# A hybrid attention block on one core: softmax sums applied to the outputs of group A instead of to its weights

## The chip, the cores and the metric

The kernel runs on one core of one Trainium2 chip. The metric is device time in microseconds, the median of several executions. The core has a matrix engine (PE, with its weight loads shown apart as PEld), a vector engine (DVE), an activation engine (ACT), a slow general engine (POOL) and a queue of transfers (SP). Matmuls write to PSUM, which is cut into banks of 512 float32 columns; ACT and DVE read them from there.

## The reference

One layer on a sequence of 1024 frames and 1024 channels, in float32. Group A (8 heads of width 64) is a chunked softmax attention, group B (8 heads) a stick-breaking attention. Both are normalised, concatenated, projected and added to the input; then comes a gated feed-forward part with a short convolution. The part that the change touches is the softmax of group A:

```
scores = einsum('bnqhd,bnkhd->bnhqk', qc, kb) * D ** -0.5
scores = where(valid, scores + bias, NEG_INF)
p = softmax(scores, axis=-1)
o = einsum('bnhqk,bnkhd->bnqhd', p, vb)
...
mixed = concatenate([rmsnorm(ya, norm_a_g), rmsnorm(yb, norm_b_g)], axis=-1)
x = x + mixed @ w_out
```

A softmax is an exponential divided by its row sum. The division may be made on the weights `p` (up to 640 for each query row and head) or on the outputs `o` (64 for each row and head); the result is the same up to rounding.

## The kernel before

The whole program runs its matmuls on PE in an order that the program itself writes out. Stages follow one another: the projections, group B, group A, the output projection, the feed-forward part. Groups A and B are latency chains between PE, DVE and ACT, so independent matmuls are put in between them, called the filler: a generator `filler()` that yields, three matmuls at a time, first the q and k projections of later head pairs (`q_p`, `k_p`, line 151), and then the half of the output projection that belongs to group B (`pb`, also line 151). The filler of the output projection comes in two halves of two weight tiles each; the second half is held back by

```
while at["qk"] < 6:
    yield None
```

and `at["qk"]` becomes 6 only when the last of the four head pairs of group A begins. What filler is left after the last block runs before the projection of group A (`pa`, line 151) starts.

A planner (`flow`) sets the order on each engine. It keeps a model clock: PE work moves the clock on (`flow.work`), chains of ACT, DVE, POOL and transfer work are emitted when the model says that their inputs are there, and when PE needs a chain that the model says is not done, `ready()` takes filler until it is. Besides, `run()` spends a planned amount of filler after each block: `cur.cost * RATES_A[p]`, where the costs of the eight blocks of a head pair add up to one, so `RATES_A` is the microseconds of filler in a head pair.

Group A has four head pairs p and eight blocks i of 128 queries in each; nk, the number of 128-key pieces, is 5, 5, 5, 5, 4, 3, 2, 1. A block goes through three steps. `scores(h)`, for each of two heads: matmuls into a bank pair (`sa`, L1058 and L1059), bias added by DVE (L1072), row maximum (L1075), exponential on ACT with the row sum as a by-product (L1089), reciprocal of the sum (L1092), and the product of the weights with it, on DVE for head 0 (L1083) and on ACT for head 1 (L1082). `turn(h)`: the weights are transposed by PE (`tpa`, L1110) and copied out by ACT (`pta`, L1114). `output`: matmuls with v (`yy`, L1123), 2 nk of them in a block. Two blocks share one bank `yy`, of which they use the first 256 columns; DVE copies these out (`yq`, L1533). The transposes and `yy` take turns in two banks. Block b's scores are issued with the transposes of block b-1 and, every other block, with the outputs of blocks b-3 and b-2.

After the last block ACT and DVE square the outputs, PE sums them (`na_ms`, L1138), ACT takes a root (with a table load, L1627), DVE a reciprocal, and PE spreads the result over the partitions (`na_rb`, L181); the `pa` results wait for that. The output weights arrive one after another through one raw tile `wo_r`: transfer, high part on ACT (L786), low part in four pieces on POOL (L129), and only then the next transfer.

Of the kernel before, what the change touches and what calls it, by code (L numbers as in the profile page):

```python
# [9 lines left out]
F32 = mybir.dt.float32  # L10
F32R = mybir.dt.float32r
BF16 = mybir.dt.bfloat16
AF = mybir.ActivationFunctionType
ALU = mybir.AluOpType
AX = mybir.AxisListType

P = 128
# [4 lines left out]
GW = 512  # L22
# [16 lines left out]
BACK, BACK_STEP = 1.0, 0.6  # L39
BEHIND_V = {"V": 1.0, "S": 5.0, "D": 7.0}  # L40
RATE_B, LEAD_B = 10.0, 4.0
RATES_A, LEAD_A = (10.0, 10.0, 10.0, 10.0), 4.0
LAG = 0.25
START = 8.0
SLACK = 0.6
# [21 lines left out]
def tile_hybrid_block(  # L67
# [14 lines left out]
    V, S, PE, GP = nc.vector, nc.scalar, nc.tensor, nc.gpsimd  # L82
# [38 lines left out]
    ident = one("ident", "ident", shape=(P, P))  # L121
# [34 lines left out]
    def cols(k):  # L156
        return slice(k * P, (k + 1) * P)
# [38 lines left out]
    with tc.tile_pool(name="kp", bufs=2) as kp:  # L196
# [13 lines left out]
        start = stage("start")  # L210
# [29 lines left out]
        for k in range(KT):  # L240
            a, b = hpair(k, "hT")
# [687 lines left out]
        HS = (A, B)  # L929
# [100 lines left out]
        class BlockA:  # L1030
# [8 lines left out]
            def scores(self, h):  # L1039
                p, i, nk = self.p, self.i, self.nk  # L1040
                qa, qb, ka, kb, la, lb = [qk_of[self.n][i] for i in range(6)]
                q, k, l = ((qa, ka, la), (qb, kb, lb))[h]
                bias, qs, nm = bias_of[p][0], cols(i), f"a{p}_{i}_{h}"
                s, mine = bigs.get(f"s{nm}")
                s = s.rearrange("p (b c) -> p b c", b=2)
                if nk == 5:
                    regions = [(s[:, b, :320], i * P + b * 320, 320) for b in range(2)]
                    full = s[:, :, :320]
                    near = s[:, 0, : 2 * P]
                elif nk == 1:  # L1050
                    regions = [(s[:, 0, : 2 * P], (i - 1) * P, 2 * P)]
                    full = near = s[:, 0, P : 2 * P]
                else:
                    regions = [(s[:, 0, : nk * P], i * P, nk * P)]
                    full = s[:, 0, : nk * P]
                    near = s[:, 0, : 2 * P]
                for o, k0, kw in regions:
                    PE.matmul(o, q[:, qs], k[:, k0 : k0 + kw], start=True, stop=False)  # L1058
                    PE.matmul(o, q[:, qs], l[:, k0 : k0 + kw], start=False, stop=True)  # L1059
                    flow.work(kw / 1200 + 0.03)  # L1060
                bb = bias[:, h, :] if nk > 1 else bias[:, h, :P]
                st = kp.tile([P, 4], F32, tag="st", name=f"st{nm}", bufs=4)
                pr = pools["sbuf"].tile([P, 5 * P], F32, tag="ws", name=f"p{nm}", bufs=3)
                self.pr[h] = pr
                po = pr[:, : nk * P]
                if nk == 5:
                    po = po.rearrange("p (b c) -> p b c", b=2)

                def mask():
                    if nk == 5:  # L1070
                        V.memset(s[0:64, 1, 256:320], NEG)
                    V.tensor_tensor(out=near, in0=near, in1=bb, op=ALU.add)  # L1072

                def top():
                    V.tensor_reduce(  # L1075
                        out=st[:, 0:1], in_=full, axis=AX.XY if nk == 5 else AX.X, op=ALU.max,
                        negate=True,
                    )

                w = nk * P  # L1080
                share = on_s(
                    w + 60, lambda: S.activation(pr[:, :w], pr[:, :w], AF.Copy, scale=st[:, 2:3])  # L1082
                ) if h else on_v(w, lambda: V.tensor_scalar(  # L1083
                    out=pr[:, :w], in0=pr[:, :w], scalar1=st[:, 2:3], scalar2=None, op0=ALU.mult
                ))
                self.chain[h] = flow.add(
                    on_v(2 * P + 100 * (nk == 5), mask),
                    on_v(w, top),
                    on_s(w + 170, lambda: S.activation(  # L1089
                        po, full, AF.Exp, bias=st[:, 0:1], accum_out=st[:, 1:2]  # L1090
                    )),
                    on_v(8, lambda: V.reciprocal(st[:, 2:3], st[:, 1:2])),  # L1092
                    share,
                    after=[bias_of[p][1]],
                )
                mine.append(self.chain[h])

            def turn(self, h):
                nk, nm = self.nk, f"a{self.p}_{self.i}"
                m = min(nk, 4)  # L1100
                ready(self.chain[h])
                if h == 0:
                    self.pt = pools["sbuf"].tile([P, 10, P], F32, tag="pt", name=f"pt{nm}")
                turns = [(f"{h}", 4 * h, [(h, b) for b in range(m)])]
                if h == 1 and nk == 5:
                    turns.append(("2", 8, [(b, 4) for b in range(2)]))
                for name, c0, parts in turns:
                    tp, mine = meds.get(f"tp{nm}_{name}")
                    for b, (src, c) in enumerate(parts):
                        PE.transpose(tp[:, cols(b)], self.pr[src][:, cols(c)], ident)  # L1110
                    flow.work(0.109 * len(parts))
                    w = len(parts)
                    o, tp = self.pt[:, c0 : c0 + w, :], tp[:, : w * P]
                    mine.append(flow.add(on_s(w * P, lambda o=o, tp=tp: S.copy(o, tp))))  # L1114
                    self.turned += mine

            def output(self, yy):
                i, nk = self.i, self.nk
# [407 lines left out]
        def collect(p, i, yy, mine):  # L1526

            r, ops = rows(i // 4), []

            def copy():  # L1530
                if i % 4 == 1:
                    yq_of[p] = kp.tile([P, GW], F32, tag="sq", name=f"yq{p}_{i}", bufs=1)
                V.tensor_copy(yq_of[p][:, (i % 4 - 1) * P : (i % 4 + 1) * P], yy[:, : 2 * P])  # L1533

            c = flow.add(on_v(2 * P, copy), after=yq_chains)
            mine.append(c)
            yq_chains[0] = c
            if i % 4 == 1:
                return
            if i == 3:  # L1540
                yh[p] = kp.tile([P, T], F32R, tag=f"y{p}", name=f"yh{p}", bufs=1)
                if p < 2:
                    yl[p] = work("wq", f"yl{p}", F32R)
                else:
                    yl[p] = kp.tile([P, T], F32R, tag="v", name=f"yl{p}", bufs=4)
                if p == 0:
                    sq_of[0] = kp.tile([P, T], F32, tag="y3", name="sq_a", bufs=1)
# [12 lines left out]
            if 0 < p < 3:  # L1560
                ops.append(on_g(GW, lambda: GP.tensor_tensor(out=sq, in0=sq, in1=yq_of[p], op=ALU.add)))
            yq_chains[0] = flow.add(*ops, after=[c])
            last_sum[p, i // 4] = yq_chains[0]

        for b in range(len(blocks) + 2):
# [34 lines left out]
            for h in range(2):  # L1600
                if cur:
                    cur.scores(h)
                if ending and h == 0 and ending.i % 2:
                    if ending.i == 1:
                        ready(*v_chains[ending.n])
                    if ending.p == 3 and ending.i == 5:
                        add_last(0)
                    yy, mine = meds.get(f"yy{ending.p}_{ending.i}")
                    for j in range(2):
                        blocks[b - 3 + j].output(yy[:, cols(j)])  # L1610
                    if ending.i == 7:
                        at["av"] = ending.n
                    collect(ending.p, ending.i, yy, mine)
                if turning:
                    turning.turn(h)
                if h:
                    run(4 * step)
# [812 lines left out]
```

## Time and profile before

| what | value |
|---|---|
| median of 3 runs | 1219.75 us (1219.66 to 1220.71) |
| the profiled execution's own time | 1221.42 us |
| span in its profile | 1219.7 us |
| PE busy | 1192.8 us, 98% |
| DVE, ACT busy | 944.7 us, 692.3 us |
| mean granted PE clock | 0.992 |

The span is the time from the first to the last instruction. A group row reads: line, engine, operation, output<-inputs, shape, count | busy time, mean of one in ns | idle time of the engine just ahead of it and who ended it. A window row reads: from:to, length, busy time (instructions) of PE, PEld, DVE, ACT and POOL, granted clock of PE, share of the transfer engines, GB/s. One matmul of float32 by float32 has two records in the trace, so 20 output matmuls of a block pair with nk = 5 and 5 are 40 records.

### The profile page before, as it was taken

How to read it: one execution, taken by the hardware profiler on the slowest of the kernel's cores; microseconds unless marked ns; L12 is line 12 of the kernel's file. 1: busy time of each engine (PE TensorE's matmuls, PEld its weight loads, DVE VectorE, ACT ScalarE, POOL GpSimd, SP SyncE). 2: the span in 40 equal slices, each digit the busy share in tenths (PEclk: the TensorE clock that was granted, in tenths of full speed). 3: DMA queues.
4: the chain of work that ended last, by engine and by line, in shares of the span. 5: the costliest groups of instructions: out<-in, count | busy, mean ns of one | idle time of the engine just before them, and what ended most of it. 6: DMA issues, size and time to landing. Idle time of an engine off the chain costs nothing.

```text
span 1219.7 us, 17426 instructions
## 1 busy us (share of the span) xinstructions
PE 1192.8 (98%) x6428; PEld 993.2 (81%) x6428; DVE 944.7 (77%) x1449; ACT 692.3 (57%) x1230; POOL 158.6 (13%) x162
## 2 busy tenths in 40 slices
PE   9999999999999989899999999999999999999997
PEld 6788888888888868688878888888888888888887
DVE  7957649888677877449997768777687779969896
ACT  7865436766677676424575555555555555444424
POOL 0001031102221110133000000000000023042036
PEclk9999999999999999999999999999999999999998
DMA  9458576777479632134032232221312196430003
GB/s 331 133 199 276 180 236 196 217 182 192 143 193 300 181 73 70 28 108 159 6 133 88 68 104 70 86 88 68 104 70 85 56 367 268 165 112 1 1 1 138
DMA packets 73651, 166.95 MB, mean 137 GB/s; under 512 B 7639, under 2 KB 23127, under 8 KB 73566
## 3 DMA queue, kind: packets, MB, share of 16 engines
q1 hardware_dynamic: 73422, 165.72, 42.5%
q8 instruction: 51, 0.84, 0.3%
q14 instruction: 34, 0.28, 0.1%
q10 hardware_dynamic: 144, 0.11, 0.0%
HBM read 118.60 MB, written 47.20 MB: 136 GB/s over the span
## 4 chain that ended last, share of the span: by engine, by line
PE 84%; DVE 6%; DMA 4%; ACT 3%; SPq 1%; issue 1%; POOL 0%; DVEq 0%; ACTq 0%; POOLq 0%
PE u_a L1845 9%; PE u_c L1845 9%; PE u_e L1845 8%; PE dz L2344 8%; PE u_b L1845 4%; PE dj L2344 4%; PE dm L2344 4%; PE v_x L503 3%; PE pa L151 3%; PE v_y L503 3%; PE yb L1008 3%; PE tpb L994 3%; PE q_p L151 2%; PE k_p L151 2%; PE yy L1123 2%; PE ee L1235 2%
## 5 line engine op out<-in xcount | busy, mean ns | idle before, releaser
L967 DVE TENSOR_TENSOR_SCAN acts<-zb,first 128x128 f32<-128x128 f32 (+7 forms) x64 | 86.5, 1351 | 18.0 <-ACT zb L976 17.8
L1869 DVE SCALAR_TENSOR_TENSOR vt<-cv,cst,vt 128x1023 f32<-128x1023 f32 (+1 forms) x44 | 58.2, 1323 | 3.4 <-ACT vt L1863 2.6
L1869 DVE SCALAR_TENSOR_TENSOR gt<-cg,cst,gt 128x1023 f32<-128x1023 f32 (+1 forms) x44 | 56.4, 1281 | 1.3 <-ACT gt L1863 0.6
L976 ACT ACTIVATE zb<-zb 128x128 f32<-128x128 f32 (+7 forms) x64 | 40.9, 640 | 26.3 <-PE zb L959 26.1
L129 POOL TENSOR_TENSOR dx_0wl<-dr,dx_0wh 128x512 fp32r<-128x512 f32 x1 | 1.4, 1371 | 412.4 <-ACT dx_0wh L2111 412.4
L1089 ACT ACTIVATE pa<-sa,sta 128x640 f32<-128x640 f32 (+4 forms) x64 | 42.6, 667 | 17.9 <-DVE sta L1075 15.4
L1863 ACT ACTIVATE gt<-cg,cst 128x1024 f32<-128x1024 f32 x22 | 27.4, 1245 | 37.1 <-DVE cg L1737 37.1
L1114 ACT COPY pta<-tpa 128x512 f32<-128x512 f32 (+3 forms) x80 | 36.4, 480 | 20.5 <-PE tpa L1110 20.2
L998 ACT COPY tb<-tpb 128x128 f32<-128x128 f32 (+3 forms) x96 | 43.0, 484 | 6.1 <-PE tpb L994 5.2
L1110 PE MATMUL tpa<-ident,pa 128*128 128x128 f32 x240 | 39.3, 284 | 5.4 <-ACT pta L1114 2.2
L994 PE MATMUL tpb<-ident,acts 128*128 128x128 f32 x288 | 43.3, 277 | 0.0
L1075 DVE TENSOR_REDUCE sta<-sa 128x1 f32<-128x640 f32 (+4 forms) x64 | 41.8, 655 | 1.4
L1734 DVE TENSOR_TENSOR up_r<-up_r 128x512 f32<-128x512 f32 x60 | 41.2, 687 | 0.8
L1110 PEld LDWEIGHTS tpa<-ident,pa 128*128 128x128 f32 x240 | 28.0, 142 | 13.9 <-ACT pta L1114 4.7
L994 PEld LDWEIGHTS tpb<-ident,acts 128*128 128x128 f32 x288 | 33.1, 140 | 6.3 <-issue 2.6
L2032 ACT COPY u_b<-u_a 128x512 f32<-128x512 f32 x19 | 10.8, 571 | 38.1 <-PE u_a L1845 38.1
L1072 DVE TENSOR_TENSOR sa<-sa,bias 128x256 f32<-128x256 f32 (+1 forms) x64 | 26.3, 413 | 6.6 <-PE sa L1059 5.3
L1123 PE MATMUL yy<-pta,v 128*64 128x128 f32 x480 | 31.3, 285 | 0.0
L1123 PEld LDWEIGHTS yy<-pta,v 128*64 128x64 f32 x480 | 27.4, 143 | 3.4 <-issue 1.6
L1008 PE MATMUL yb<-tb,dv 128*64 128x128 f32 x448 | 29.2, 273 | 0.0
L1658 POOL TENSOR_TENSOR n_acc<-n_acc,n_sq 128x384 f32<-128x384 f32 (+2 forms) x23 | 24.1, 1047 | 28.9 <-ACT n_sq L1657 28.2
L129 POOL TENSOR_TENSOR wo_l<-wo_r,wo_h 128x256 fp32r<-128x256 f32 x28 | 20.1, 749 | 59.3 <-ACT wo_h L786 59.3
(1394 smaller groups left out, 4038.8 us busy)
## 6 DMA issues: line engine op xcount, KB each, us to landing
up_r<-in_w_up_dram SPq DMA_DIRECT2D x44, 512.0 KB, 3.6
act<-vt SPq DMA_DIRECT2D x22, 512.0 KB, 2.6
dr<-in_w_dn_dram SPq DMA_DIRECT2D x20, 512.0 KB, 7.5
dr<-act SPq DMA_DIRECT2D x20, 512.0 KB, 6.6
wv<-in_w_v_dram SPq DMA_DIRECT2D x16, 256.0 KB, 5.4
xin<-in_xT_dram SPq DMA_DIRECT2D x16, 256.0 KB, 5.4
row<-in_x_rows_dram SPq DMA_DIRECT2D x16, 256.0 KB, 2.6
raw<-in_w_in_dram SPq DMA_DIRECT2D x8, 512.0 KB, 5.3
```

The source lines that it names most:

```text
L151: PE.matmul(o, w[:, sl], t[:, rows(g)], start=first and i == 0, stop=last and i == 2,)
L503: PE.matmul(bank[j], t[:, cols(j)], w, start=p in (1, 5) and k == 0 and i == 0, stop=k == 3 and i == 2, skip_group_check=True,)
L967: V.tensor_tensor_scan(out=a[:, :w], data0=z, data1=first[:, :w], initial=1.0, op0=ALU.mult, op1=ALU.max,)
L994: PE.transpose(tp[:, cols(b)], self.a[h][:, cols(b0 + b)], ident)
L998: mine.append(flow.add(on_s(m * P, lambda o=o, tp=tp: S.copy(o, tp))))
L1008: PE.matmul(yy[HS[h], :], (d if j else v)[:, off : off + 64], self.at[h][:, self.c0[h] + j * P : self.c0[h] + (j + 1) * P], start=j == 0, ...
L1089: on_s(w + 170, lambda: S.activation(po, full, AF.Exp, bias=st[:, 0:1], accum_out=st[:, 1:2])),
L1110: PE.transpose(tp[:, cols(b)], self.pr[src][:, cols(c)], ident)
L1123: PE.matmul(yy[HS[h], :], v[:, (i + c) * P + h * 64 : (i + c) * P + (h + 1) * 64], self.pt[:, 4 * h + c if c < 4 else 8 + h, :], start=c = ...
L1845: PE.matmul(o, w[:, cols(k)], t, start=start and k == 0 and i == 0, stop=k == 3 and i == 2, skip_group_check=True,)
L1869: V.scalar_tensor_tensor(out=t[:, : T - lag], in0=o[:, lag:], scalar=c1(c + ct), in1=t[:, : T - lag], op0=ALU.mult, op1=ALU.add,)
L2344: PE.matmul(o[m], w[:, cols(m)], t, start=i in (0, 1, 4, 5) and p == ps_[0] and j == 0, stop=p == ps_[-1] and j == 2, skip_group_check=True,)
```

## The change

The exponentials are no longer multiplied. The row sums of both heads of a block stand in one small tile (`self.st`, six columns: two maxima, two sums, two reciprocals), and one reciprocal serves both. Where the outputs of two blocks are made, a new step `spread` comes ahead of them: for each block and head one matmul whose stationary operand is the column of reciprocals, read 64 times over, and whose moving operand is the identity. It writes the reciprocals, spread over the 64 partitions of the head, to columns 256 to 511 of the same bank `yy`. ACT copies these 256 columns to SBUF (`rq`), and DVE's copy of the outputs becomes a product with them. `RATES_A` goes from 10 to 8.

```
--- before.py
+++ after.py
@@ -39,7 +39,7 @@
 BACK, BACK_STEP = 1.0, 0.6
 BEHIND_V = {"V": 1.0, "S": 5.0, "D": 7.0}
 RATE_B, LEAD_B = 10.0, 4.0
-RATES_A, LEAD_A = (10.0, 10.0, 10.0, 10.0), 4.0
+RATES_A, LEAD_A = (8.0, 8.0, 8.0, 8.0), 4.0
 LAG = 0.25
 START = 8.0
 SLACK = 0.6
@@ -1059,7 +1059,9 @@
                     PE.matmul(o, q[:, qs], l[:, k0 : k0 + kw], start=False, stop=True)
                     flow.work(kw / 1200 + 0.03)
                 bb = bias[:, h, :] if nk > 1 else bias[:, h, :P]
-                st = kp.tile([P, 4], F32, tag="st", name=f"st{nm}", bufs=4)
+                if not h:
+                    self.st = kp.tile([P, 6], F32, tag="st", name=f"st{nm}", bufs=4)
+                st = self.st
                 pr = pools["sbuf"].tile([P, 5 * P], F32, tag="ws", name=f"p{nm}", bufs=3)
                 self.pr[h] = pr
                 po = pr[:, : nk * P]
@@ -1073,26 +1075,23 @@
 
                 def top():
                     V.tensor_reduce(
-                        out=st[:, 0:1], in_=full, axis=AX.XY if nk == 5 else AX.X, op=ALU.max,
+                        out=st[:, h : h + 1], in_=full, axis=AX.XY if nk == 5 else AX.X, op=ALU.max,
                         negate=True,
                     )
 
                 w = nk * P
-                share = on_s(
-                    w + 60, lambda: S.activation(pr[:, :w], pr[:, :w], AF.Copy, scale=st[:, 2:3])
-                ) if h else on_v(w, lambda: V.tensor_scalar(
-                    out=pr[:, :w], in0=pr[:, :w], scalar1=st[:, 2:3], scalar2=None, op0=ALU.mult
-                ))
                 self.chain[h] = flow.add(
                     on_v(2 * P + 100 * (nk == 5), mask),
                     on_v(w, top),
                     on_s(w + 170, lambda: S.activation(
-                        po, full, AF.Exp, bias=st[:, 0:1], accum_out=st[:, 1:2]
+                        po, full, AF.Exp, bias=st[:, h : h + 1], accum_out=st[:, 2 + h : 3 + h]
                     )),
-                    on_v(8, lambda: V.reciprocal(st[:, 2:3], st[:, 1:2])),
-                    share,
                     after=[bias_of[p][1]],
                 )
+                if h:
+                    self.scale = flow.add(
+                        on_v(8, lambda: V.reciprocal(st[:, 4:6], st[:, 2:4])), after=self.chain
+                    )
                 mine.append(self.chain[h])
 
             def turn(self, h):
@@ -1113,6 +1112,15 @@
                     o, tp = self.pt[:, c0 : c0 + w, :], tp[:, : w * P]
                     mine.append(flow.add(on_s(w * P, lambda o=o, tp=tp: S.copy(o, tp))))
                     self.turned += mine
+
+            def spread(self, rr):
+                flow.need(self.scale)
+                for h in range(2):
+                    PE.matmul(
+                        rr[HS[h], :], self.st[:, 4 + h : 5 + h].to_broadcast([P, 64]), ident,
+                        start=True, stop=True, skip_group_check=True,
+                    )
+                flow.work(0.11)
 
             def output(self, yy):
                 i, nk = self.i, self.nk
@@ -1530,9 +1538,17 @@
             def copy():
                 if i % 4 == 1:
                     yq_of[p] = kp.tile([P, GW], F32, tag="sq", name=f"yq{p}_{i}", bufs=1)
-                V.tensor_copy(yq_of[p][:, (i % 4 - 1) * P : (i % 4 + 1) * P], yy[:, : 2 * P])
-
-            c = flow.add(on_v(2 * P, copy), after=yq_chains)
+                V.tensor_tensor(
+                    out=yq_of[p][:, (i % 4 - 1) * P : (i % 4 + 1) * P], in0=yy[:, : 2 * P],
+                    in1=x["t"][:, : 2 * P], op=ALU.mult,
+                )
+
+            def spread():
+                x["t"] = kp.tile([P, GW], F32, tag="tmp", name=f"rq{p}_{i}", bufs=3)
+                S.copy(x["t"][:, : 2 * P], yy[:, 2 * P :])
+
+            x = {}
+            c = fs.chain(on_s(2 * P, spread), on_v(2 * P, copy), then=yq_chains, slack=0.0)[1]
             mine.append(c)
             yq_chains[0] = c
             if i % 4 == 1:
@@ -1606,6 +1622,8 @@
                     if ending.p == 3 and ending.i == 5:
                         add_last(0)
                     yy, mine = meds.get(f"yy{ending.p}_{ending.i}")
+                    for j in range(2):
+                        blocks[b - 3 + j].spread(yy[:, cols(2 + j)])
                     for j in range(2):
                         blocks[b - 3 + j].output(yy[:, cols(j)])
                     if ending.i == 7:
```

The planner's order then moves. Names in the rows: `sa_i_h` scores, `tpa_i_h` transposes, `yy_i` outputs of blocks i-1 and i, `sta` the sums, `pb` filler. PE, head pair 2, around blocks 4 and 5, before:

```order
L1110 MATMUL tpa_3_1_4800<-ident,pa_3_1_4757 128x128 x4
L1110 MATMUL tpa_3_2_4806<-ident,pa_3_0_4708 128x128
L1110 MATMUL tpa_3_2_4806<-ident,pa_3_1_4757 128x128
L1058 MATMUL sa_5_0_4809<-ka_4256,qa_3991 128x384
L1059 MATMUL sa_5_0_4809<-la_4333,qa_3991 128x384
L1123 MATMUL yy_3_4816<-pta_2_4739,v_3628 64x128 x10
L1123 MATMUL yy_3_4816<-pta_3_4776,v_3628 64x128 x10
L1110 MATMUL tpa_4_0_4849<-ident,pa_4_0_4775 128x128 x4
```

and the same place now:

```order
L1109 MATMUL tpa_3_2_4644<-ident,pa_3_1_4573 128x128
L151 MATMUL pb_1_4648<-yh_4229,wo_h 128x512
L151 MATMUL pb_1_4648<-yl_4230,wo_h 128x512
L151 MATMUL pb_1_4648<-yh_4229,wo_l 128x512
L151 MATMUL pb_1_4648<-yh_4231,wo_h 128x512
L151 MATMUL pb_1_4648<-yl_4232,wo_h 128x512
L151 MATMUL pb_1_4648<-yh_4231,wo_l 128x512
L1058 MATMUL sa_5_0_4660<-ka_3952,qa_3878 128x384
L1059 MATMUL sa_5_0_4660<-la_4063,qa_3878 128x384
L1119 MATMUL yy_3_4668<-ident,sta_2_0_4460 64x128 x2
L1119 MATMUL yy_3_4668<-ident,sta_3_0_4519 64x128 x2
L1131 MATMUL yy_3_4668<-pta_2_4556,v_3603 64x128 x10
```

Filler now stands where there was none. In the whole list the filler matmuls of head pairs 0, 1, 2 and 3 and of the part between the last `yy` and the first `pa` number 78, 72, 42, 66 and 30 before, and 48, 36, 63, 45 and 96 now: the sum is 288 both times. All 42 of head pair 2 stood ahead of the scores of its block 3. Of the 96 at the end 54 stand ahead of the first `na_rb`.

ACT, from the last transposes of group A to the root, before:

```order
L1114 COPY pta_7_5420<-tpa_7_1_5436 128x128
L1556 ACTIVATE yh_5289<-yq_5_5411,cst 128x512
L1558 ACTIVATE yq_5_5411<-yq_5_5411 128x512
L786 CAST wo_h<-wo_r 128x1024 x2
L1627 ACT_TABLE_LOAD
L1153 ACTIVATE rn_79<-rn_79,eps 128x8
L1162 COPY rba<-na_rb 128x512 x2
```

and now:

```order
L1113 COPY pta_7_5283<-tpa_7_1_5297 128x128
L1548 COPY rq_7_5319<-yy_7_5299 128x256
L786 CAST wo_h<-wo_r 128x1024
L1572 ACTIVATE yh_5162<-yq_5_5277,cst 128x512
L1574 ACTIVATE yq_5_5277<-yq_5_5277 128x512
L786 CAST wo_h<-wo_r 128x1024
L1645 ACT_TABLE_LOAD
L1161 ACTIVATE rn_79<-rn_79,eps 128x8
```

Two weight tiles are still split ahead of the root, but they are one place earlier in the list of weights (the fourth and fifth of eight, before the fifth and sixth).

More of the change, by code (lines that the diff above doesn't have):

```diff
@@ L41 @@
 RATE_B, LEAD_B = 10.0, 4.0
-RATES_A, LEAD_A = (10.0, 10.0, 10.0, 10.0), 4.0
+RATES_A, LEAD_A = (8.0, 8.0, 8.0, 8.0), 4.0
 LAG = 0.25
@@ L1061, in scores @@
                 bb = bias[:, h, :] if nk > 1 else bias[:, h, :P]
-                st = kp.tile([P, 4], F32, tag="st", name=f"st{nm}", bufs=4)
+                if not h:
+                    self.st = kp.tile([P, 6], F32, tag="st", name=f"st{nm}", bufs=4)
+                st = self.st
                 pr = pools["sbuf"].tile([P, 5 * P], F32, tag="ws", name=f"p{nm}", bufs=3)
@@ L1075, in top @@
                     V.tensor_reduce(
-                        out=st[:, 0:1], in_=full, axis=AX.XY if nk == 5 else AX.X, op=ALU.max,
+                        out=st[:, h : h + 1], in_=full, axis=AX.XY if nk == 5 else AX.X, op=ALU.max,
                         negate=True,
@@ L1080, in scores @@
                 w = nk * P
[L1081 to L1085, printed above, removed]
                 self.chain[h] = flow.add(
@@ L1089, in scores @@
                     on_s(w + 170, lambda: S.activation(
-                        po, full, AF.Exp, bias=st[:, 0:1], accum_out=st[:, 1:2]
+                        po, full, AF.Exp, bias=st[:, h : h + 1], accum_out=st[:, 2 + h : 3 + h]
                     )),
-                    on_v(8, lambda: V.reciprocal(st[:, 2:3], st[:, 1:2])),
-                    share,
                     after=[bias_of[p][1]],
                 )
+                if h:
+                    self.scale = flow.add(
+                        on_v(8, lambda: V.reciprocal(st[:, 4:6], st[:, 2:4])), after=self.chain
+                    )
                 mine.append(self.chain[h])
@@ L1115, in turn, with spread @@
                     self.turned += mine
+            def spread(self, rr):
+                flow.need(self.scale)
+                for h in range(2):
+                    PE.matmul(
+                        rr[HS[h], :], self.st[:, 4 + h : 5 + h].to_broadcast([P, 64]), ident,
+                        start=True, stop=True, skip_group_check=True,
+                    )
+                flow.work(0.11)
             def output(self, yy):
@@ L1532, in copy, with spread @@
                     yq_of[p] = kp.tile([P, GW], F32, tag="sq", name=f"yq{p}_{i}", bufs=1)
-                V.tensor_copy(yq_of[p][:, (i % 4 - 1) * P : (i % 4 + 1) * P], yy[:, : 2 * P])
-            c = flow.add(on_v(2 * P, copy), after=yq_chains)
+                V.tensor_tensor(
+                    out=yq_of[p][:, (i % 4 - 1) * P : (i % 4 + 1) * P], in0=yy[:, : 2 * P],
+                    in1=x["t"][:, : 2 * P], op=ALU.mult,
+                )
+            def spread():
+                x["t"] = kp.tile([P, GW], F32, tag="tmp", name=f"rq{p}_{i}", bufs=3)
+                S.copy(x["t"][:, : 2 * P], yy[:, 2 * P :])
+            x = {}
+            c = fs.chain(on_s(2 * P, spread), on_v(2 * P, copy), then=yq_chains, slack=0.0)[1]
             mine.append(c)
@@ L1608, in tile_hybrid_block @@
                     yy, mine = meds.get(f"yy{ending.p}_{ending.i}")
+                    for j in range(2):
+                        blocks[b - 3 + j].spread(yy[:, cols(2 + j)])
                     for j in range(2):
```

## Prediction

> **What bounds the kernel now.** I read the page first, for the engine that is busy all the time and for the chain that ended last.
>
> ```profile
> PE 1192.8 (98%) x6428; PEld 993.2 (81%) x6428; DVE 944.7 (77%) x1449; ACT 692.3 (57%) x1230; POOL 158.6 (13%) x162
> PE 84%; DVE 6%; DMA 4%; ACT 3%; SPq 1%; issue 1%; POOL 0%; DVEq 0%; ACTq 0%; POOLq 0%
> ```
>
> PE is the bound: 26.9 us of 1219.7 are not PE. An engine like that is made faster only by less work on it or by closing its gaps, so the next view is the busy time by stretch, for PE alone. The first stretch begins with the first scores of group A, the second lies in head pair 2 behind the output of block 1, the fourth begins with the last outputs, the fifth with the spreading of the norm.
>
> ```profile
> core 0: us, PE busy (x), PEclk, DMA share, GB/s
> 334.24:435.16 100.92, 97.76 (x722) 1.00 0.82 222
> 435.16:460.00 24.84, 18.79 (x166) 0.86 0.14 46
> 460.00:501.20 41.20, 40.87 (x324) 1.00 0.11 40
> 501.20:515.22 14.02, 8.81 (x51) 0.93 0.14 37
> 515.22:522.00 6.78, 6.78 (x24) 0.63 0.28 77
> ```
>
> Two stretches hold most of the gaps: 24.84 - 18.79 = 6.05 us and 14.02 - 8.81 = 5.21 us. The other two of group A hold 3.16 + 0.33 = 3.5 us. The column of the granted clock shows a second loss: PE works at 0.86 of its clock in the second stretch and at 0.63 behind the second gap. I price it as busy time times the missing share, 18.79 x 0.14 = 2.6 us and 6.78 x 0.37 = 2.5 us. In steps of 2 us one sees where it comes from:
>
> ```profile
> 442.00:444.00 2.00, 0.36 (x3) 1.00 0.67 254
> 444.00:446.00 2.00, 0.86 (x5) 0.77 0.02 6
> 446.00:448.00 2.00, 2.00 (x11) 0.50 0.00 0
> 448.00:450.00 2.00, 2.00 (x36) 0.87 0.04 8
> ```
>
> PE was busy for 0.36 + 0.86 of 4 us; then the clock was halved for some 3 us. The Trainium skill, "TensorE: Matmul & The Clock Gate", section on the HAM clock gate, says that the clock halves after an idle window of about 3.4 us; here it fell with PE a third busy, so the measurement decides, and waits close to each other cost clock as well. By the page alone the 2.6 us would not be there to win, and the time would be 2.6 us higher.
>
> Who ended the gaps, from the view of waits (total, times, longest):
>
> ```profile
> PE na_rb L181 <- DVE rn L1154: 5.2, 1, 5.2
> PE sa L1058 <- ACT pa L1089: 3.1, 2, 1.6
> PE tpa L1110 <- ACT pta L1114: 2.2, 3, 1.6
> PE tpa L1110 <- ACT pa L1082: 1.6, 2, 1.1
> PE tpa L1110 <- DVE yq L1533: 1.2, 2, 0.7
> ```
>
> The one long gap is the wait for the norm of group A. The others are latencies of the softmax chain where no filler stands between: in head pair 2 all 42 filler matmuls stand ahead of block 3, and the next ones are let go only with head pair 3. The chain of waits in front of the long gap reads:
>
> ```profile
> 504.63 1.05 ACT wo_h L786
> 505.75 2.83 POOL wo_l L129 x4
> 508.59 3.57 DMA wo_r<-in_w_out_dram
> 512.18 1.04 ACT wo_h L786
> 513.25 1.28 ACT L1627
> 514.54 0.31 ACT rn L1153
> 514.87 0.21 DVE rn L1154
> 515.22 1.94 PE na_rb L181 x8
> ```
>
> The root stands on ACT behind two weight tiles; the second waits for its transfer, that one for POOL to be done with the tile before. Their sum is 10.3 us, and PE had 30 filler matmuls for it.
>
> **The change part by part.** The prices:
>
> ```profile
> 400.56 3.43 PE pb L151 x15
> 404.46 0.66 PE tpa L1110 x6
> 476.81 2.33 PE yy L1123 x40
> L1082 ACT ACTIVATE pa<-pa,sta 128x640 f32<-128x640 f32 (+4 forms) x32 | 22.3, 696 | 5.1 <-DVE sta L1092 5.0
> L1083 DVE TENSOR_SCALAR pa<-pa,sta 128x640 f32<-128x640 f32 (+4 forms) x32 | 16.0, 500 | 0.8
> L1089 ACT ACTIVATE pa<-sa,sta 128x640 f32<-128x640 f32 (+4 forms) x64 | 42.6, 667 | 17.9 <-DVE sta L1075 15.4 <-DVE sta L1092 1.8
> L1089 ACT ACTIVATION_READ_ACCUMULATOR pa<-sa,sta 128x1 f32 x64 | 12.9, 201 | 0.0
> L1092 DVE RECIPROCAL sta<-sta 128x1 f32<-128x1 f32 x64 | 10.2, 159 | 14.5 <-ACT pa L1089 14.1
> L1114 ACT COPY pta<-tpa 128x256 f32<-128x256 f32 x24 | 9.1, 379 | 4.8 <-PE tpa L1110 4.7
> L1533 DVE COPY yq<-yy 128x256 f32<-128x256 f32 x16 | 6.7, 416 | 4.0 <-PE yy L1123 4.0
> ```
>
> *Removed:* 22.3 us of ACT, 16.0 us of DVE, half of the 64 reciprocals (5.1 us). Neither engine is the bound, so this gives no PE time by itself; it takes a product (0.50 or 0.70) and a reciprocal (0.16) out of the way from an exponential to its transposes. *Added off PE:* 16 ACT copies of 256 columns, by L1114 0.38 us each, 6.1 us; DVE's copy becomes a product of the same size, which I take at its 0.42. Both engines end with less work, hidden under PE as now; without that cover the 6.1 us of copies would be the price.
>
> *Added on PE:* two matmuls for each of 32 blocks, 128 records, with 64 stationary columns and 128 moving ones like `yy`. That row gives 2.33 / 40 = 0.058 us a record, so 7.5 us, all of it on the path. The stationary operand is one column read 64 times, which no row of that width shows; the upper bound is the pace of the transposes, 0.66 / 6 = 0.11, 14.1 us. Below 7.5 no row leads. I take 7.5, since the shape is that of `yy`.
>
> *Moved:* 66 filler matmuls of 3.43 / 15 = 0.229 us go from the head pairs to the end; their sum of work stays. In head pair 2 there are now 33 between the scores of block 3 and those of block 7, 7.5 us of work where 6.05 us were idle: -6.05 - 2.6 = -8.7. At the end 54 stand between the last outputs and the spreading, 12.4 us. The root's way is now: copy 0.38, weight tile 1.05, POOL 2.83, transfer 3.57, weight tile 1.04, table 1.28, root 0.31, reciprocal 0.21, together 10.7 us. The gap closes with 1.7 us to spare: -5.2 - 2.5 = -7.7. Past it the next thing that could be late is the weight tile for the second column pair of `pa`: the one ahead of it is split only behind the two norm copies on ACT, then come POOL 2.83, a transfer 3.57, ACT 1.04 and POOL 2.83 once more, against 30 filler and 24 `pa` matmuls (12.4 us); about even, and I put nothing on it. SP's loads of q and k for head pairs 2 and 3 move too, since their projections end later: the last k projection now ends at block 2 of head pair 2, six blocks ahead of the scores that need it, so I price the loads themselves at nothing; what is queued behind them is priced below.
>
> *New waits:* one bank holds outputs and spread reciprocals. ACT's copy comes ahead of DVE's product, so the bank is held 0.38 us longer after the last output matmul, if the copy waits for that matmul; if it ran as soon as the two spreading matmuls are done, it would be nothing. I take the dearer end, since both halves are one tile. Behind the copy on ACT stand transposes' copies and the next exponential. In five of the 16 pairs (blocks 1 and 7 of head pairs 0 and 1, block 1 of head pair 3) no filler stands between `yy` and the transposes that need its bank: 5 x 0.38 = 1.9 us. The other new wait comes over SP:
>
> ```profile
> DVE bias L1019 <- DMA bias<-in_toep_dram: 2.1, 2, 1.1
> ```
>
> DVE stops for the bias table of the next head pair, with row maxima behind it. In head pair 1 that load now stands behind seven pieces of q and k and a weight tile, and filler is thinnest there (36 matmuls in place of 72): I add one wait of 1.1 us. Bounds for both together: -3.5, if the shorter chain also closes the small gaps, and +8, if every pair waits half a microsecond.
>
> The Trainium skill, "PSUM — Partial Sum Buffer", section on bank collisions, says that two engines must not touch one bank and quadrant at once and that software has to guard by the bank; so the copy cannot run under the output matmuls of the same bank. No row before shows such a pair. If it did run under them, the 1.9 us would fall away and the time be 1212.0.
>
> **Sum:** 7.5 - 8.7 - 7.7 + 3.0 = -5.9 us. The profiled execution took 1221.42 us, 1.7 outside its span; less 5.9 that is 1215.5. It lies 1.67 above the median of the runs, so the median to come is 1213.9.
>
> **The rivals.** *The bank decides (slower).* When `yy` ends ACT may be inside an exponential (0.67) and its sum (0.20); copy and product then come that much later, and with them the transposes that need the bank. At 0.87 in each of 16 pairs that is 13.9 instead of the 1.1 above: 7.5 - 16.4 + 13.9 + 1.9 = +6.9, 1226.7. It decides from 8.9 us of new waits, 0.56 a pair. For it: 1.2 us are lost at this place today, with an engine less in the chain. Against it: eleven pairs have filler there, three matmuls (0.69 us) at least or the end of the group. *The spreading costs what transposes cost:* 14.1 in place of 7.5, 1220.4, no change. Against it: 64 columns, as in `yy`. *The root is late all the same,* because POOL or a transfer slips by more than the 1.7 us to spare; with the whole gap kept it would be -8.7 + 7.5 + 3.0 = +1.8, 1221.5, no change. That is the case in which the filler kept back doesn't do its work. *All gaps close:* 7.5 - 16.4 - 3.5 = -12.4, 1207.3; for it speaks the shorter chain, against it the thin filler.
>
> **How the numbers follow.** Forecast 0.63, with a range of its own from 1208 to 1217.3; all gaps close 0.13; spreading dear 0.07; root late 0.06; bank 0.11. What this kernel's measurement can tell from no change is 0.2%, 2.4 us. Faster: 0.63 + 0.13 = 0.76. Same: 0.13. Slower: 0.11. The range is 1207 to 1220.5: below, all gaps closed; above, +8 us of new waits (1218.9) and most of the two cases without change.
>
> **What would show it.** In the profile of the changed kernel: `yy<-ident,sta` with about 0.058 us a record and 7.5 us in all; no wait of `na_rb` for `rn` over 1 us, and a clock of 1.00 behind it; head pair 2 with under 2 us idle; waits of L1109 for `yq` near 2 to 3 us. The forecast is wrong if waits of transposes for `yq` or for copies sum to more than 9 us, or if the clock falls in head pairs 0 and 1, where the filler is now thinnest.

## The result, and the profile after

The change made the kernel faster: 1215.3 us median (1214.19 to 1217.33, 6 runs) against 1219.7 (1217.6 to 1221.41, 6 runs), a ratio of 0.9965 with a 95% interval of 0.9952 to 0.9978. The prediction was 1213.9. In a later series of runs it came to 1216.4, a ratio of 0.9966 (0.9953 to 0.9978); what follows compares the experiments with that series.

The engine line of the page of the changed kernel, whose profiled execution took 1215.3 us with a span of 1213.4:

```profile
PE 1195.3 (99%) x6556; PEld 995.4 (82%) x6556; DVE 929.7 (77%) x1385; ACT 677.5 (56%) x1214; POOL 161.9 (13%) x162
```

PE has 128 records more and is busy 2.5 us longer, while the span is 6.3 us shorter: its idle time fell from 26.9 to 18.1 us. The stretches of group A begin with its first scores, the first outputs of head pair 2, the last transposes of that pair, the first `na_rb` and the first `pa` (columns: stretch, its length, PE busy and records, granted clock, DMA share, GB/s). The first two are those of the prediction within 1 us of the program; the third holds its third and fourth.

```profile
core 0: us, PE busy (x), PEclk, DMA share, GB/s
335.62:421.46 85.84, 83.21 (x700) 1.00 0.70 195
421.46:448.99 27.53, 26.47 (x237) 1.00 0.75 191
448.99:500.87 51.88, 51.61 (x411) 1.00 0.12 42
500.87:512.98 12.11, 10.73 (x51) 1.00 0.51 173
512.98:522.00 9.02, 9.02 (x41) 1.00 0.40 116
```

The stretch of head pair 2, 6.05 us idle at a clock of 0.86 before, has 27.53 - 26.47 = 1.06 us idle at full clock. Nothing is idle just ahead of `na_rb`, and the clock behind it is 1.00 where it was 0.63. What is left stands in the view of waits of PE for group A (total, times, longest):

```profile
PE tpa L1109 <- DVE yq L1541: 1.8, 1, 1.8
PE pb L151 <- DVE x L1207: 1.4, 1, 1.4
PE tpa L1109 <- ACT pta L1113: 0.9, 1, 0.9
PE sa L1058 <- ACT pa L1086: 0.7, 4, 0.2
```

No `na_rb` is in that list any more. By the timelines of ACT, DVE and PE the root was done in time:

```profile
497.72 1.28 ACT L1645 ACT_TABLE_LOAD   x1
499.01 0.30 ACT L1161 ACTIVATE rn<-rn,eps 128x8 f32<-128x8 f32 x1
499.35 0.20 DVE L1162 RECIPROCAL rn<-rn 128x8 f32<-128x8 f32 x1 [0.94 <-ACT rn L1161]
500.87 0.60 PE L181 MATMUL na_rb<-ident,rn 128*128 128x128 f32 x4
```

The reciprocal ended at 499.55, 1.3 us ahead of its reader. The price is in the chain that ended last: in front of each pair's outputs now stand eight spreading records,

```profile
481.12 0.59 PE yy L1119 x8
481.71 1.53 PE yy L1131 x28
```

and the same 28 output records before:

```profile
496.55 1.68 PE yy L1123 x28
```

0.59 + 1.53 - 1.68: this pair costs 0.44 us more, 16 of them 7.0.

### The profile page after: what moved, and what is told of

It is laid out like the page before. It is cut to its first block, busy times and chain, and to the rows that moved or that the text cites. A ratio compares the mean times of both kernels' runs of the same rounds, so it can differ in the third digit from the quotient of the medians.

```text
span 1213.4 us, 17634 instructions
## 1 busy us (share of the span) xinstructions
PE 1195.3 (99%) x6556; PEld 995.4 (82%) x6556; DVE 929.7 (77%) x1385; ACT 677.5 (56%) x1214; POOL 161.9 (13%) x162
## 4 chain that ended last, share of the span: by engine, by line
PE 89%; DVE 5%; ACT 2%; DMA 2%; issue 1%; SPq 0%; POOL 0%; DVEq 0%; ACTq 0%; POOLq 0%
PE u_c L1863 9%; PE u_e L1863 9%; PE u_a L1863 9%; PE dz L2362 8%; PE u_b L1863 5%; PE dj L2362 4%; PE dm L2362 4%; PE v_x L503 4%; PE pb L151 4%; PE pa L151 3%; PE k_p L151 3%; PE v_y L503 3%; PE yb L1008 2%; PE q_p L151 2%; PE yy L1131 2%; PE tpb L994 2%
## 5 line engine op out<-in xcount | busy, mean ns | idle before, releaser
L1109 PEld LDWEIGHTS tpa<-ident,pa 128*128 128x128 f32 x240 | 27.5, 140 | 10.9 <-ACT pta L1113 3.8
L2050 ACT COPY u_b<-u_a 128x512 f32<-128x512 f32 x19 | 10.9, 571 | 38.1 <-PE u_a L1863 38.1
L151 PE MATMUL pb<-yh,wo_h 128*128 128x512 f32 x64 | 26.6, 415 | 1.4 <-DVE x L1207 1.4
```

The lines of the kernel that those rows point to most:

```text
L151: PE.matmul(o, w[:, sl], t[:, rows(g)], start=first and i == 0, stop=last and i == 2,)
```

## The experiments

All times are medians. "Group A" is the stretch from the first scores of A to the first `pa` in the profiled execution; its start differs by up to 1.6 us between kernels whose program ahead of it has the same order (the last section), so group A is read for itself. The kernels that start it near 334 have some 1.4 us on the change that their edits did not make, in the one execution that was profiled of each; for them the medians and the lengths of A do not differ by the same amounts.

| kernel | us | ratio to before (95%) | A starts | length of A | PE idle in A | clock |
|---|---|---|---|---|---|---|
| before | 1219.9 | | 334.24 | 182.57 | 14.76 | 0.97 |
| the change | 1216.4 | 0.9966 (0.9953-0.9978) | 335.42 | 177.32 | 5.32 | 1.00 |
| spread twice | 1222.0 | 1.0009 (1.0000-1.0018) | 333.87 | 183.77 | 4.96 | 1.00 |
| copy twice | 1219.0 | 0.9989 (0.9980-0.9998) | 334.00 | 182.60 | 8.94 | 0.99 |
| `x_6`, `x_7` early | 1214.0 | 0.9950 (0.9936-0.9963) | 334.10 | 175.59 | 3.88 | 1.00 |
| 30 ahead of `na_rb` | 1218.4 | 0.9989 (0.9980-0.9999) | 334.15 | 181.07 | 7.54 | 0.99 |
| filler alone, on demand | 1227.6 | 1.0062 (1.0050-1.0074) | 333.83 | 189.30 | 17.07 | 0.96 |
| filler alone, even | 1224.5 | 1.0040 (1.0027-1.0053) | 333.90 | 186.14 | 16.48 | 0.99 |
| early loads, cover | 1213.7 | 0.9949 (0.9937-0.9961) | 335.19 | 175.93 | 4.35 | 1.00 |
| copy on DVE | 1216.5 | 0.9974 (0.9965-0.9983) | 334.02 | 178.49 | 5.70 | 1.00 |
| copy on DVE, early loads | 1214.4 | 0.9956 (0.9943-0.9968) | 333.95 | 177.12 | 4.61 | 1.00 |
| early loads, more filler early | 1213.4 | 0.9950 (0.9937-0.9962) | 335.26 | 176.26 | 4.80 | 1.00 |

**The change once more**, no edit.

> The changed kernel once more, as the base that the next three are compared with. Expected: 1215.3 us as before, 4.4 us (0.36%) less than the kernel before. It also shows which of the small waits that the trace of the change had in group A come back in a second execution: those of transposes for `yq` (1.8 us, once) and of `pb` for `x` (1.4 us, once). What comes back at the same place belongs to the program's order, the rest is chance.

Measured 1216.4, 1.1 us more than expected: medians of one kernel differ by that much between two series, and smaller differences of medians are not read below. All four waits above came back with the same sizes. They belong to the program's order, and each is worth asking after.

**The spreading twice.**

```diff
-                for h in range(2):
+                for h in (0, 1, 0, 1):
                     PE.matmul(
```

> Each of the spreading matmuls is issued twice, 128 records more on PE and nothing else moved. Theory of the prediction (0.058 us a record, all of it on the path): +7.5 us, about 1222.8, so that the gain is used up and 3 us more. Rival, the spreading is dear (0.11 us a record, as the transposes): +14, 1229. Rival, the spreading lies in latency in which PE would wait anyway: +0 to 3, 1215 to 1218.

Measured 1222.0, 5.6 us above the change. The stretch of group A, of the change and of this kernel:

```profile
335.42:512.74 177.32, 172.00 (x1393) 1.00 0.52 148
```

```profile
333.87:517.64 183.77, 178.81 (x1522) 1.00 0.51 143
```

A is 6.45 us longer and PE 6.8 us longer busy: 0.050 to 0.053 us a record, nearly all of it on the path. The rival of spreading at the price of transposes (14 us) is out, and so is the one of spreading in the shadow of latency. Doubled, the spreading uses up the whole gain: 1222.0 against 1219.9 before.

**The copy twice.**

```diff
                 S.copy(x["t"][:, : 2 * P], yy[:, 2 * P :])
+                S.copy(x["t"][:, : 2 * P], yy[:, 2 * P :])
```

> ACT's copy of the spread reciprocals is made twice, so the bank of outputs is held some 0.38 us longer in each of the 16 pairs, and `yq` comes that much later; the order on PE stays. Theory of the prediction (only in the few pairs where no filler stands between the outputs and the transposes does PE feel it): +0.4 to +1.9 us, 1215.7 to 1217.2; the low end if, as in the trace of the change, a single pair is short of cover. Rival, the bank decides: 16 x 0.38 = +6 us, 1221.

Measured 1219.0, 2.6 us above the change, between the 1.9 at most of the theory and the 6 of the rival. In the profiled execution A is 5.3 us longer and starts 1.4 us earlier. The waits of PE in A, and the stretches around the longest of them:

```profile
PE tpa L1109 <- ACT pta L1113: 5.8, 6, 2.4
PE pb L151 <- DVE x L1207: 1.4, 1, 1.4
PE sa L1058 <- ACT pa L1086: 1.4, 4, 0.3
```

```profile
356.00:358.00 2.00, 1.45 (x7) 0.64 0.54 162
358.00:360.00 2.00, 2.00 (x8) 0.50 0.00 0
```

and the same place in the change:

```profile
356.00:358.00 2.00, 0.35 (x3) 1.00 1.09 371
358.00:360.00 2.00, 2.00 (x14) 1.00 0.34 100
```

PE idles 8.94 us in A in place of 5.32. Half of the difference does not come through the copy. In head pair 1 a wait of 1.83 us opened where the change has none, and ahead of it DVE had stood still for the bias table, with the row maximum, the exponential and the copies queued behind (the timelines of DVE and PE):

```profile
391.27 0.35 DVE L1019 TENSOR_SCALAR bias<-bias,cst 128x256 f32<-128x256 f32 x1 [1.69 <-DMA bias<-in_toep_dram]
394.62 0.87 PE L1109 MATMUL tpa<-ident,pa 128*128 128x128 f32 x6 [1.83 <-ACT pta L1113]
```

That table landed 11.1 us after its issue; in the two executions of the change it took 7.7 and 6.3. Why is not shown, and nothing in the trace ties it to the copy. The other 1.8 us of idle time are waits for copies of transposes, which stand behind the second copy on ACT, and, in four blocks, scores that wait 0.34 us in place of 0.18. A last 1.7 us are clock: the wait in head pair 0 grew from 1.83 to 2.36 us, and behind it the clock was halved for some three microseconds, which the shorter wait had not cost. So the second copy itself lengthens A by some 3.5 us: more than the theory allowed, less than the rival. The copy fits once, without a margin of its own length. Whether the bank is short or ACT's queue is not separated: at the wait in head pair 0 the product that empties the bank ends at 356.47 and the copy of transposes at 356.50.

**Two loads in their old place.**

```diff
-                for d in ds:
+                for d in (4, 5, 6, 7) if dp == 2 else ds:
                     if d not in x2:
                         load_x2(d)
```

> The last two residual tiles `x_6` and `x_7` of group A are loaded ahead of the raw weight tiles on SP's queue, in the place that they had before the change; the order on PE stays. In the trace of the change SP issued them behind the weight tiles, whose first waits for its buffer, and PE waited 1.4 us for the additions that need them, with PE's busy share at 3.62 of 5 us there. Theory (a cost of the moved loads that the prediction put at nothing): -1.4 us, 1213.9, and no wait of `pb` for `x`. Rival, the wait for the tiles hides another (a weight tile that comes later now, or the roots): no change, 1215.3, with the 1.4 us put down to something else at the same place.

Measured 1214.0 (1213.39 to 1214.75, against 1214.91 to 1216.83 for the change): 2.4 us less where 1.4 were expected. The timeline of SP's queue in the change shows the reason:

```profile
492.43 8.54 SPq L770 DMA_DIRECT2D wo_r<-in_w_out_dram  x2
501.02 0.90 SPq L1215 DMA_DIRECT2D x<-in_xT_dram  x2
```

The two loads of `x` stood behind a weight tile that waited for its buffer, and landed 5.4 us after their issue, when `pb` wanted its bank emptied by the additions to them. With the loads ahead, that wait is gone and nothing took its place there: A is 1.7 us shorter. Of the 2.4 us between the medians the trace puts another 1.3 on the earlier start of A, and takes back part at the end of the program, where a late group of matmuls, `dj`, now waits 0.9 us for ACT. The first is the theory; the other two are not explained by the edit.

**The gap before `na_rb` put back.**

```diff
-TAIL_A = (6, 8, 4)
+TAIL_A = (6, 0, 4)
```

> The change with 30 filler matmuls ahead of the first `na_rb` in place of 54, as before the change; the other 24 stand behind the second `na_rb`. In the trace of the change the reciprocal of the root ended 1.5 us before PE came to `na_rb`; without 24 x 0.229 = 5.5 us of filler PE has to wait 4.0 us. Theory of the prediction (gap and half clock behind it): +4.0 + 2.5, less up to 1.4 for the wait for `x`, which may vanish in the gap: +5.1 to +6.5, 1221 to 1222.5, with a granted clock well under 1 in the first 7 us behind `na_rb`. Rival, the gap alone counts and no clock is lost: +2.6 to +4.0, 1219 to 1220. Rival, the filler kept back is not what closed the gap: 0.

Measured 1218.4, 2.0 us above the change and below both ranges that were expected; A is 3.75 us longer and starts 1.3 us earlier. Its wait, and the stretch from `na_rb` to `pa`:

```profile
PE na_rb L181 <- DVE rn L1162: 3.5, 1, 3.5
```

```profile
497.71:515.22 17.51, 17.51 (x75) 0.90 0.36 121
```

The gap is 3.5 us, the clock behind it costs 17.51 x 0.10 = 1.8, and the wait of 1.4 for `x` vanishes in the gap: 3.9, near the 3.75 measured. The filler in front of `na_rb` does what the prediction said, with a smaller price of the clock than the 2.5 before.

**The filler without the division**, dealt out on demand. The kernel before, with a budget on what a softmax chain may pull:

```diff
-                while not c.done or c.t > flow.now + 0.3:
+                while (not c.done or c.t > flow.now + 0.3) and budget[0] > 0:
                     us = next(fill, None)
...
                     done[0] += us
+                    budget[0] -= us
...
                 n, p = cur.n, cur.p
+                budget[0] = (48, 36, 63, 45)[p] * 0.68 / 3 - 0.1
```

> The softmax of before (weights divided, no spreading, no copy), but with the filler of the change: 54, 36, 63, 51 in the head pairs and 84 at the end, 54 of them ahead of `na_rb`. Within a head pair the first blocks take it, as in the kernel before. Theory 1 (the filler's new places bring the gain and the division only costs): the gap before `na_rb` goes with its clock, -7.7, and that of head pair 2 at least in part, up to -8.7: 1203.5 to 1212. Theory 2 (the shorter chain is what lets filler leave the head pairs): the head pairs lose 54 x 0.229 = 12.4 us of cover under a chain that is as long as before, so PE idles there nearly as much more, clock beside it: 1219 to 1226, with new waits for ACT's product `pa` L1082 or for the exponential.

Measured 1227.6, slower than before by 0.6% and 1.6 us beyond the range of theory 2. The two longest waits of PE in A:

```profile
PE sa L1058 <- ACT pa L1089: 5.6, 4, 1.4
PE tpa L1110 <- ACT pa L1082: 5.0, 6, 1.4
```

The wait for the norm is gone here too, and yet A is 6.7 us longer: the exponential and the product hold PE up in the later blocks of the head pairs that gave filler away, and where such waits follow closely the clock falls:

```profile
399.00:408.00 9.00, 7.16 (x62) 0.81 0.80 299
408.00:416.00 8.00, 5.89 (x44) 0.79 0.00 1
488.00:492.00 4.00, 2.36 (x12) 0.73 0.00 0
492.00:500.00 8.00, 7.88 (x59) 0.71 0.00 0
```

Theory 1 is out for this dealing.

**The same, dealt out evenly.** The demand gets nothing, and the rates deal: `RATES_A = (10.9, 8.2, 14.3, 10.2)`, budget 0.4 in each head pair.

> The same, but the filler of a head pair is dealt out evenly behind each block in place of on demand: 48, 36, 63, 54 and 87, with 60 ahead of `na_rb`. Theory 1: 1203.5 to 1212, as for the run with the demand. Theory 2: 1215 to 1226; each block's chain has one product more to wait for, so waits of transposes for `pa` come in nearly every block; if only the uneven dealing was to blame in the run with the demand, this one is faster than that by several us and near the change (1215).

Measured 1224.5, still slower than before. The longest waits are more in number:

```profile
PE tpa L1110 <- ACT pa L1082: 5.7, 9, 1.9
PE sa L1058 <- ACT pa L1089: 3.5, 5, 1.2
PE tpa L1110 <- DVE yq L1535: 2.8, 5, 1.7
```

The uneven dealing was 3 us of the loss, not its cause. So the filler does not win alone, in either dealing: at nearly the same places of the filler the division is worth 1224.5 - 1216.4 = 8 us against even dealing, after paying for its spreading. The other half alone, the division with the filler left where it was, was not run, and neither was moving only as much filler as the gap before `na_rb` needs. The rate in the diff, 10 to 8, does nothing in the old kernel, which has the same order of instructions on every engine with either; the change with 10 was not run. That the filler moved because the shorter chains pull less of it is what the planner's rule says; no run shows it by itself. (The idle time explains 1.7 of the 3.6 us by which A is longer than before; what fills the rest of PE's busy time here stays open.)

**Cover for the longest wait left.** With the early loads:

```diff
+                if h and cur and cur.p == 0 and cur.i == 3:
+                    for _ in range(3):
+                        done[0] += next(fill) or 0.0
                 if turning:
                     turning.turn(h)
```

> The change with two edits: `x_6` and `x_7` loaded ahead of the weight tiles (1214.0 in the run before), and nine filler matmuls (2.1 us) placed ahead of the transposes that waited 1.8 us for `yq` in head pair 0, where ACT loads two tables. The rest of the filler shifts with it: 63, 51, 45, 45 and 84, with 54 ahead of `na_rb`. Theory (that wait is one place without cover): 1.8 us less, 1212.2. Rival (in the place that the filler left a gap of the same size opens, in head pair 2 above all, where there are 45 in place of 63): no change, 1214.

Measured 1213.7, A 0.3 us longer than with the early loads alone: the rival. The waits:

```profile
PE tpa L1109 <- ACT pta L1113: 1.7, 3, 1.4
PE pb L151 <- DVE x L1207: 1.5, 1, 1.5
```

The wait for `yq` is gone; one of 1.4 us for a copy of transposes opened further on in the same head pair (at 359.9), and `pb`, which now begins earlier, waits for a tile of `x` in head pair 2 (at 414). It opened elsewhere than the rival had said, but it opened.

**The copy on DVE**, so that it need not stand behind ACT's table loads.

```diff
-                S.copy(x["t"][:, : 2 * P], yy[:, 2 * P :])
+                V.tensor_copy(x["t"][:, : 2 * P], yy[:, 2 * P :])
...
-            c = fs.chain(on_s(2 * P, spread), on_v(2 * P, copy), ...
+            c = fs.chain(on_v(2 * P, spread), on_v(2 * P, copy), ...
```

> The change with the copy of the spread reciprocals on DVE in place of ACT (16 copies of some 0.4 us); the scheduler moves a little filler with it (57 in place of 63 in head pair 2, 102 in place of 96 at the end; 54 ahead of `na_rb` as in the change). The run with two copies on ACT cost 5.3 us within group A, and PE's new waits there were for ACT's copies of the transposes `pta`, so ACT's queue looks like the price, not the bank. If it is ACT's queue: -1 to -2 us, 1214.4 to 1215.4, the wait of 1.8 us for `yq` in head pair 0 gone, since DVE need not wait for the table loads. If it is the bank, whichever engine empties it: no change. If DVE's own queue (row maxima, the mask) is as tight as ACT's: +2 or more, with new waits for the exponential `pa`.

Measured 1216.5, no difference from the change.

```profile
PE pb L151 <- DVE x L1207: 2.4, 2, 1.4
PE tpa L1109 <- ACT pta L1113: 1.8, 2, 0.9
PE sa L1058 <- ACT pa L1086: 1.1, 5, 0.4
```

The wait for `yq` went as expected, and others grew by as much or more: A is 1.2 us longer, and starts 1.4 us earlier. The time is the one expected if the bank decides, but no wait is left for `yq`, the product that empties it: they are for copies of transposes, for exponentials and for `x`, which `pb` now awaits a second time. So the copy cost no less on DVE, and what sets its price stays open. A product that reads both halves from the bank would need no copy; the Trainium skill, "PSUM — Partial Sum Buffer", section "Specifications (TRN2)", says that a VectorE instruction may take at most one tensor input from PSUM, which no run here shows.

> The same, with `x_6` and `x_7` loaded ahead of the weight tiles. If both gains stand and add: 1212 to 1213, the fastest so far. If the copy on DVE brings nothing: 1214.0, as with the loads alone.

Measured 1214.4: the early loads bring 2.1 us here, about as much as with the copy on ACT, and the copy on DVE brings nothing.

**Early loads and rates of 14, 14, 8, 8.**

> The change with `x_6` and `x_7` loaded early and the rates 14, 14, 8, 8, which deal the filler 63, 60, 45, 45 and 75: more of it in head pairs 0 and 1, 54 ahead of `na_rb` as in the change, 21 behind it in place of 42. If the small waits in group A are places without cover that more filler closes: -1 to -2 against 1214.0. If head pair 2 with 45 in place of 63 opens its gaps again, or the weight tile for the second column pair of `pa` comes late with 21 matmuls less ahead of it: +1 to +4.

Measured 1213.4 (1213.15 to 1214.2), A 176.26: no gain in A over the early loads alone, and no loss either: as in the run with the cover, `pb` begins earlier and waits for a tile of `x`, 1.7 us here. With 45 in place of 63 filler matmuls head pair 2 stayed closed, and 21 less behind `na_rb` did not make the weight tile late. Four kernels with the early loads lie between 1213.4 and 1214.4; I cannot tell them apart, and all of them beat the change.

## Why the prediction was right

It said faster, with 1213.9 for the time, and the three terms that carry it came out close to their sizes. The stretches of group A as a whole, before (with the one behind `na_rb`) and then in the change:

```profile
334.24:516.81 182.57, 167.81 (x1265) 0.97 0.51 141
515.22:516.81 1.59, 1.59 (x8) 0.50 0.00 0
```

```profile
335.62:512.98 177.36, 172.02 (x1393) 1.00 0.53 148
```

- **Spreading, +7.5.** Doubled, it cost 6.5 to 6.8. The first one, from PE's busy time in A with the clock put back that was lost there before (2.6 in head pair 2 and 1.59 x 0.5 = 0.8 at `na_rb`), comes to 172.02 - 167.81 + 3.4 = 7.6. (The product of a stretch's busy time and its mean clock is rough: summed over steps of 2 us, head pair 2 lost 3.0 us to the clock, which makes this 8.0 and the next term -8.0.) The row of the output matmuls was the right one to take; that the broadcast column costs anything of its own does not show.
- **Head pair 2, -8.7.** 6.05 - 1.06 = 5.0 us of gap and 2.6 of clock went: -7.6. One wait of 0.9 for a copy of transposes was left, where I had left nothing. (The stretch's clock is in the page; no run put this gap back by itself.)
- **The gap before `na_rb`, -7.7.** 5.2 us of gap and the clock behind it went. The time to spare was 1.3 us for 1.7 forecast, and with only 30 matmuls in front a gap of 3.5 us and a lower clock came back. The next thing that I feared, the weight tile for `pa`, waited nowhere, not even with 21 filler matmuls less.
- **New waits, +3.0.** This term failed in its places. Of the five pairs in which `yy` was to hold PE up 0.38 us longer, one is in the trace, in head pair 0; there PE had waited nearly as long before, for a copy of transposes, as the two timelines of PE show (before, then the change):

```profile
357.88 0.44 PE L1110 MATMUL tpa<-ident,pa 128*128 128x128 f32 x2 [1.58 <-ACT pta L1114]
```

```profile
357.65 0.87 PE L1109 MATMUL tpa<-ident,pa 128*128 128x128 f32 x6 [1.83 <-DVE yq L1541]
```

  The bank is not shown to be what held PE there: the product ended at 357.59 and a copy of transposes at 357.63. DVE's waits for the bias table fell from 2.1 to 0.5 us in all, none of them passed on to PE, where I had added 1.1; the risk was real, since in the run with two copies a late table cost PE 1.8. And a wait that I had priced at nothing came: 1.4 us for `x`, because "SP's loads move too" had been asked only of q, k and bias, not of the tiles of `x` behind a waiting weight tile. Outside the two large gaps PE idled 14.76 - 6.05 - 5.21 = 3.5 us before and 5.34 - 1.06 = 4.3 now, +0.8 in place of +3.0. The smallness was in part luck: the second copy cost A some 3.5 us, late table left out, where the same reasoning gave 1.9.
- **Sum.** In A: 7.6 - 7.6 - 5.2 - 0.8 + 0.8 = -5.2, which is the difference of the two lengths. That it comes out is no test, because the 7.6 was read from PE's busy time in the same two stretches; the tests are the doubled spreading and the 30 matmuls. Behind A it is 2.4 us less. The clock explains 1.7 of them: before, the first 10 us there ran at 0.83, and in the change at 1.00.

```profile
516.81:526.81 10.00, 10.00 (x39) 0.83 0.34 95
```

  Ahead of A it is 1.4 more, which no term of mine had. Together -6.2 of the 6.3 us between the spans, where I had -5.9.

The medians differ by less, 4.4 and 3.5 us, which is three quarters and three fifths of the 5.9 forecast. The profiled execution of before lay 1.7 us above its median, that of the change at its own; which of the terms was larger in that one execution no run here tells. The later start of A is as large as the miss, 1215.3 for 1213.9, but only the two profiled executions of the change show it.

The rivals: the root was not late, the spreading not dear, not all gaps closed. The bank did not decide, but with less room than the prediction's argument ("eleven pairs have filler there") implied. In that rival's recorded sum the 1.1 for the bias table and the 1.9 for the bank have changed places: it should be 7.5 - 16.4 + 13.9 + 1.1 = +6.1 and 1225.9, which changes nothing else. A rival that I did not have, filler that wins without the division, was worth asking and lost in both dealings that were run.

## What to carry to other kernels

Where one engine is always busy, a shorter chain on the other engines is worth the filler that it no longer needs: here it could be carried to the places that were short of it, while nearly the same move under the old chain lost 5 to 8 us. When work is moved, read every in-order queue behind it by its last entry too: a load that merely changed places with a waiting one cost 1.4 us, and one line gave it back. And when a wait is covered with filler in a program this full, look where the filler came from before counting the gain.

## What the runs showed of the hardware

**DVE behind POOL.** The order of the program ahead of group A is the same in all these kernels, yet A starts at 334 or at 335.4. The timelines of DVE and POOL in the change, and then in the kernel with early loads:

```profile
312.10 2.75 DVE L1019 TENSOR_SCALAR bias<-bias,cst 128x256 f32<-128x256 f32 x2
314.77 0.94 DVE L967 TENSOR_TENSOR_SCAN acts<-zb,first 128x384 f32<-128x384 f32 x1
312.17 2.53 POOL L1459 TENSOR_TENSOR y<-y,y 128x1024 f32<-128x1024 f32 x1 [28.00 <-ACT y L1457]
```

```profile
311.72 0.61 DVE L1019 TENSOR_SCALAR bias<-bias,cst 128x256 f32<-128x256 f32 x2
313.31 1.42 DVE L971 TENSOR_TENSOR acts<-acts 128x127 f32<-128x127 f32 x1
312.05 2.53 POOL L1459 TENSOR_TENSOR y<-y,y 128x1024 f32<-128x1024 f32 x1 [27.99 <-ACT y L1457]
```

In both a DVE instruction ends 0.15 us behind POOL's sum of two tiles: the two scalings, 0.61 us elsewhere, take 2.75, or the product, 0.29 elsewhere, takes 1.42. In the change the block fell on the earlier instruction, and PE waited 1.2 us for the scan behind it. Not every DVE instruction is held: in the other kernel a scan of 128x384 ran beside POOL in 0.96 us, 0.94 elsewhere. Which one is hit goes with the head start of DVE's scalings on POOL: 0.03 to 0.24 us in the four executions that start A after 335 (the change twice, the cover, the last run), 0.31 to 0.60 in the nine others. This matches the Trainium skill, "SBUF — State Buffer", section "SBUF: two separate sides": the ports that DVE and GpSimd (POOL) share are an exclusive lock held for a whole instruction, and the other side is blocked. Why the head start differs is not shown.

**The clock.** A gap of 1.83 us in head pair 0 cost no clock, one of 2.36 at the same place halved it, and so did one of 3.5 ahead of `na_rb`. The length of a gap alone does not decide: with the filler dealt out evenly, a gap of 1.89 us that ended at 384.68 was followed by a clock of 0.50 from 385.59 to 389.00, while one of 1.96 us in head pair 0 of the last run was followed by none. The Trainium skill, "TensorE: Matmul & The Clock Gate", section on the HAM clock gate, has an idle window of about 3.4 us; here less was enough.
